# Mixer B: one product with v per four score tiles, 512 columns wide, and put-off work moved to the end of a step

## The chip, the cores and the metric

The kernel runs on one core of a Trainium2 chip. The metric is the device time of one launch in microseconds (us); three runs of the kernel before gave 1504.79, 1506.16 and 1506.5 us, median 1506.16. A core has engines that each work through a list of instructions in order and wait for each other by semaphores: TensorE (PE, matmuls and transposes; PEld is its loading of the stationary operand), VectorE (DVE), ScalarE (ACT), GpSimd (POOL), and SyncE (SP), which here only issues DMAs. [...]

## What is computed

Two layers over 1024 tokens of width 1024: layer 0 with neighbourhood attention (mixer A), layer 1 with grouped-query attention (mixer B), each followed by a dense part (output projection, gated per-layer embedding). The change is in mixer B:

```python
def q_block(qb):                                    # 128 queries, 16 heads, 4 k/v heads
    sc = jnp.einsum('bkgqd,bksd->bkgqs', qb, k).astype(jnp.float32) * scale
    pr = jax.nn.softmax(sc, axis=-1).astype(v.dtype)
    return jnp.einsum('bkgqs,bksd->bkgqd', pr, v)
...
return (o * jax.nn.silu(gate)) @ w_out
```

Every product of float32 accuracy is made of two or three products of rounded operands: an operand x is split into a high part xh (rounded to fp32r) and a rest xl = x - xh.

## The kernel before

The phases run one after the other: mixer A, a dense phase, mixer B, a dense phase. In mixer B (`mixer_b`, lines 1054 to 1382) the attention is 128 steps (`steps`, line 1253). A step is one tile of 128 queries of one head against all 1024 keys: 16 heads in 8 pairs, two halves of the tokens (`hf`), four tiles t in each half, so that four steps in a row belong to one head and half. Each step has three parts:

- `f_S` (scores): four matmuls of 512 columns into a PSUM tile of 128x1024 (two such tiles take turns), and on DVE the minimum of each row, `mn` (line 1265).
- `f_E` (exp): one ACTIVATE on ACT over 128x1024 into P (line 1271), with the sum of each row.
- `f_T`: eight transposes of P on PE (line 1281) into two PSUM tiles of four blocks (`psT` has two buffers, so the transposes of the next step wait until these are read), each copied by ACT to PTh (line 1283) and with the rest taken by DVE to PTl (line 1284).

The parts overlap over steps: the program text of step n holds f_T of n, f_E of n+1 and f_S of n+2. PTh and PTl hold two tiles (256 columns). At every second step, n = 2, 4, 6, ..., `f_AV` (line 1289) multiplies V with both kept tiles: 8 matmuls with PTh and 8 with PTl, each 256 columns wide, into one half of a 512-column PSUM tile `o`. Such a step is called an AV step here, any other a plain step. In an AV step the order is f_AV, f_E, f_T, f_S; in a plain step f_T, f_E, f_S. After the fourth tile `head_end` puts off the work that brings `o` to SBUF (lines 548 and 512). In the middle of some AV steps (`turned`, line 1295) `q_stack` transposes the queries of the next two heads; the copy that brings a head's queries to the rows of the stationary operand QS follows later in two parts, on ACT (line 1244) and on DVE (line 1245).

Between the parts of the steps stands dense work: pieces of projections (q, k and v of later heads, gates, embedding products), 6 matmuls of 512 columns or 12 of 256 each. `mix` (line 372) places them: each entry of the list `att` carries a weight (CB for an AV step, CN for a plain step: weights of turn, f_AV, f_T, f_E, f_S), and after each entry pieces are issued until their share of the total equals the share of the weights done. A step of kind "apart" is given a piece ahead of it if none has come since the last f_T. What brings a piece's PSUM to SBUF (`leave`) may be put off behind the f_E that follows it.

`pulse` (line 351) is called after every entry of `att`. It does two things: `WQ.pump` moves the queue of weights on (a DMA to a staging buffer, then a copy `wh` on ACT, line 230, and the rest `wl` on DVE, line 235; new ones begin only while `WQ.gate` is true, which is between the scores of an odd step and the next `turn`), and `post.tick` counts down all other put-off work (copies, row scalings, DMAs of results) and issues what is due. With `turn`, f_AV, f_E, f_T and f_S as entries a plain step has four pulses and an AV step five.

The 128 steps are given to `mix` in four groups of 32 (g = 0 to 3). By the code group 0 has 24 dense pieces, group 1 has 50, groups 2 and 3 have 32 each. `WQ.gate` is None (always open) from step 112.

Of the kernel before, what the change touches and what calls it, by code (L numbers as in the profile page):

```python
# [12 lines left out]
F32R = mybir.dt.float32r  # L13
# [8 lines left out]
NT = 8  # L22
# [6 lines left out]
SEED = 0x5F3759DF - (1 << 22) - (1 << 31)  # L29
WSLOTS = 4  # L30
CA = (1.0, 0.5, 1.25, 1.0, 0.75)
CB = (1.25, 1.0, 2.0, 0.5, 1.0)
CN = (1.5, 0.0, 1.0, 1.0, 1.5)
DG, DR, DQ, DY, NP = 1, 2, 2, 1, 8
KT, KN = 2, 4
# [125 lines left out]
def trunk(ctx, tc, x, wts, rpb, gains, hgains, mask, sides, rope, gain0, out):  # L161
    nc = tc.nc
# [119 lines left out]
    def load_y(l, t):  # L282
        for i, (d, src) in enumerate(zip((HTh, HTl), yD[l])):
            k0 = 4 if i and t >= 4 else 0
            (act if t < 4 and l else sync).dma_start(d[:, t, k0:7].bitcast(F32), src[t, :, k0:7])
# [34 lines left out]
    def mm(ps, a, b, first, last):  # L320
        pe.matmul(ps, a, b, start=first, stop=last, skip_group_check=True)  # L321
# [29 lines left out]
    def pulse():  # L351
        WQ.pump()
        post.tick()
# [16 lines left out]
    leave = Evac()  # L370
# [683 lines left out]
    def mixer_b(pend):  # L1054
        with ExitStack() as es:
# [3 lines left out]
            one = es.enter_context(tc.tile_pool(name="bone", bufs=1))  # L1059
# [3 lines left out]
            psT = es.enter_context(tc.tile_pool(name="bpt", bufs=2, space=PSUM))  # L1063
            psO = es.enter_context(tc.tile_pool(name="bpo", bufs=1, space=PSUM))

            PTh = one.tile([128, NT, 256], F32R, name="PTh")
            PTl = one.tile([128, NT, 256], F32R, name="PTl")

            def dalloc():
                if pro[0]:  # L1070
# [8 lines left out]
            KA, KB, V, QT, QST, P, RS, OP = {}, {}, {}, {}, {}, {}, {}, {}  # L1079
# [150 lines left out]
            def q_stack(pair, hf):  # L1230
                g = pair // 2
                ps = psT.tile([128, 4, 128], F32, name="t")
                c = slice((pair % 2) * 128, (pair % 2) * 128 + 128)
                for t in range(4):
                    pe.transpose(ps[:, t], QT[g, hf][:, t, c], ident)  # L1235
                raw = sb.tile([128, 512], F32, name="th")
                act.activation(raw, ps.rearrange("p t c -> p (t c)"), AF.Copy)
                for j in range(2):
                    own, oth = slice(64 * j, 64 * j + 64), slice(64 - 64 * j, 128 - 64 * j)
                    qs = sb.tile([128, 512], F32R, name="QS", bufs=3)  # L1240
                    QST[2 * pair + j, hf] = qs

                    def high(qs=qs, own=own, oth=oth):
                        act.activation(qs[own], raw[own], AF.Copy)
                        post.add(DQ, lambda: dve.tensor_tensor(qs[oth], raw[own], qs[own], ALU.subtract))
                    if pro[0]:
                        high()
                    else:
                        post.add(QO[j], high)
# [3 lines left out]
            steps = [(2 * p + j, hf, t) for p in range(8) for hf in range(2) for j in range(2) for t in range(4)]  # L1253

            def f_S(h, hf, t):
                g = h // 4
                ps = psS.tile([128, 1024], F32, name="s")
                qt = QST[h, hf][:, t * 128:(t + 1) * 128]
                for kk, kt in enumerate((KA[g], KB[g])):
                    for c in range(2):  # L1260
                        mm(ps[:, c * 512:(c + 1) * 512], qt, kt[:, c * 512:(c + 1) * 512], kk == 0, kk == 1)
                if t == 0:
                    RS[h, hf] = sb.tile([128, 4], F32, name="rs", bufs=3)
                mn = sb.tile([128, 1], F32, name="mn", bufs=3)
                dve.tensor_reduce(mn, ps, axis=AX.X, op=ALU.min)  # L1265
                P[h, hf, t] = (ps, mn)
# [6 lines left out]

            def f_T(h, hf, t):
                p = P.pop((h, hf, t))
                c = slice((t % 2) * 128, (t % 2) * 128 + 128)
                for b in range(2):
                    ps = psT.tile([128, 4, 128], F32, name="t")
                    for i in range(4):
                        k = 4 * b + i  # L1280
                        pe.transpose(ps[:, i], p[:, k * 128:(k + 1) * 128], ident)  # L1281
                    ks = slice(4 * b, 4 * b + 4)
                    act.activation(PTh[:, ks, c], ps, AF.Copy)  # L1283
                    dve.tensor_tensor(PTl[:, ks, c], ps, PTh[:, ks, c], ALU.subtract)  # L1284
# [1 line left out]
            def talloc():  # L1286
                return psO.tile([128, 512], F32, name="o").rearrange("p (t c) -> p t c", t=4)

            def f_AV(h, hf, t):
                if t == 1:  # L1290
                    OP[h, hf] = psO.tile([128, 512], F32, name="o")
                o = OP[h, hf][:, (t - 1) * 128:(t + 1) * 128]
                for k in range(NT):
                    mm(o, V[h // 4][:, k], PTh[:, k], t == 1 and k == 0, False)
                while turned:
                    turned.pop(0)()
                for k in range(NT):
                    mm(o, V[h // 4][:, k], PTl[:, k], False, t == 3 and k == NT - 1)
                if t == 3:
                    fin = head_end(sb, h, hf, RS[h, hf], OP.pop((h, hf)), ylive, 1, gg, talloc)  # L1300
                    if fin:
                        later.add(FIN[1], fin)
# [18 lines left out]
            def exps(n):  # L1321
                def f():
                    f_E(*steps[n])
                f.first = True
                return f

            def blocks(n):
                def f():
                    f_T(*steps[n])
                f.kind = "apart" if n % 2 else "blocks"  # L1330
                return f
            for g in range(4):
                att = []
                for n in range(32 * g, 32 * g + 32):
                    h, hf, t = steps[n]
                    av = n >= 2 and n % 2 == 0
                    w = CB if av else CN
                    def turn():
                        if WQ.gate:
                            WQ.gate = False  # L1340
                        later.tick()
                    att.append((turn, w[0]))
                    if av:
                        att.append((lambda n=n: f_AV(*steps[n - 1]), w[1]))
                    te = [(blocks(n), w[2])]
                    if n + 1 < len(steps):
                        te.append((exps(n + 1), w[3]))
                    if n % 2 == 0 and n > 0:
                        te.reverse()
                    att += te  # L1350
                    if n + 2 < len(steps):
                        def scores(n=n):
                            f_S(*steps[n + 2])
                            WQ.gate = n % 2 == 1 if n < 112 else None
                        att.append((scores, w[4]))
                    m = n + QS_AT
                    if m % 8 == 0 and m < len(steps):
                        hn, fn, _ = steps[m]
                        att.append((lambda hn=hn, fn=fn: turned.append(lambda: q_stack(hn // 2, fn)), 0.0))
                    if YLOAD_B <= n < YLOAD_B + NT:  # L1360
                        att.append((lambda t=n - YLOAD_B: load_y(1, t), 0.0))
                if g == 3:
                    att.append((lambda: f_AV(*steps[-1]), CB[1]))
                def gates(p):
                    return [i for hf in range(2) for i in gate_items("bg", p, hf, dalloc, sb, gg)]
                dense = []
                if g > 0:
                    dense += left
                if g < 3:
                    qi = q_items(g + 1, pool)  # L1370
                    kv = kv_items(1, pool) if g == 1 else [None, None]
                    dense += kv[:-2] + qi[:KS] + [k for k in kv[-2:-1] if k] + qi[KS:8] + [k for k in kv[-1:] if k] + gates(2 * g + 1) + qi[8:]
                    left = gates(2 * g + 2)
                else:
                    WQ.cap[3] = 2
                    dense += gates(2 * g + 1) + pp_items(1, dalloc, sb, TAGS_B)
                mix(att, dense, hold=HOLD + 1 if g == 3 else 0)
# [442 lines left out]
    mixer_a()  # L1820
    pend = dense_phase(0)
    mixer_b(pend)
    dense_phase(1)

# [17 lines left out]
```

## Time and profile before

| | |
|---|---|
| runs, median (lowest to highest) | 1506.16 us (1504.79 to 1506.5) |
| the profiled execution's own time | 1505.39 us |
| its span, first to last instruction | 1503.6 us |
| PE, DVE, ACT, POOL busy | 98%, 71%, 61%, 31% of the span |
| granted TensorE clock | 0.999 |
| mixer B's 128 steps in the trace | about 762.6 to 1321.6 us |

The span is shorter than the execution by 1.8 us, which lie before its first and behind its last instruction. A busy PE is not PE at its peak, since the ends of pipelined matmuls are modelled; the distance between the starts of matmuls tells how fast PE goes. All rows with times are of this one execution.

### The profile page before, as it was taken

The page shows a single profiled execution, that of the slowest core. Times are in us where ns is not written, and L with a number is a line of the kernel's source. Part 1 is how long each engine was busy: PE and PEld are TensorE (multiplying, and loading weights), DVE is VectorE, ACT ScalarE, POOL GpSimd, SP SyncE. Part 2 cuts the span into 40 slices and gives each one's busy share as a digit, 9 for nine tenths or more (in the row PEclk, how much of TensorE's full clock was granted, in tenths as well). Part 3 has the DMA queues.
Part 4 walks back from the last instruction along what each step waited for, and adds up shares of the span by engine and source line. Part 5 has one row for each costly group of instructions (what it writes and reads, how often), then busy time and mean ns, then how long its engine had stood idle before and what let it go on. Part 6 is the DMA issues. An engine that isn't in the chain of part 4 may idle for free.

```text
span 1503.6 us, 24725 instructions
## 1 busy us (share of the span) xinstructions
PE 1480.6 (98%) x8885; PEld 1304.0 (87%) x8885; DVE 1071.6 (71%) x2042; ACT 917.2 (61%) x1866; POOL 461.0 (31%) x623
## 2 busy tenths in 40 slices
PE   8999999999999999999999999999999999999998
PEld 8888988988988887888988999989999988888886
DVE  7566476477477598756887786777877887689844
ACT  7676476477477535433567776767767777745432
POOL 1456476387265200020322222443131300000123
PEclk9999999999999999999999999999999999999999
DMA  8334374283122863262210111111101122763223
GB/s 257 126 104 131 71 178 139 64 168 100 36 89 85 326 247 99 92 206 80 77 50 22 33 51 39 47 33 44 58 28 48 38 78 66 240 234 114 69 90 135
DMA packets 91242, 157.44 MB, mean 105 GB/s; under 512 B 18160, under 2 KB 54256, under 8 KB 90608
## 3 DMA queue, kind: packets, MB, share of 16 engines
q1 hardware_dynamic: 87120, 143.53, 29.1%
q0 software_dynamic: 2560, 8.39, 3.7%
q10 hardware_dynamic: 1440, 3.94, 0.8%
q8 instruction: 71, 1.16, 0.3%
q14 instruction: 51, 0.42, 0.1%
HBM read 125.30 MB, written 50.83 MB: 117 GB/s over the span
## 4 chain that ended last, share of the span: by engine, by line
PE 51%; DVE 7%; ACT 2%; issue 1%; POOL 0%; ACTq 0%; POOLq 0%; DVEq 0%
PE d L321 25%; PE s L321 9%; PE o L321 8%; PE t L1281 7%; PE t L496 1%; DVE xn L1616 1%; PE t L321 1%; DVE X L1512 1%; DVE PTl L1284 1%; DVE HTl L1458 0%; DVE wl L235 0%; DVE mn L1265 0%; DVE wl L1410 0%; PE t L1235 0%; ACT wh L230 0%
## 5 line engine op out<-in xcount | busy, mean ns | idle before, releaser
L321 PE MATMUL d<-wh,HTh 128*128 128x256 f32 (+1 forms) x1000 | 331.8, 335 | 1.9 <-DVE X L1512 0.6
L321 PE MATMUL d<-wh,HTl 128*128 128x256 f32 (+1 forms) x1000 | 327.7, 331 | 0.4 <-DVE HTl L498 0.4
L321 PE MATMUL d<-wl,HTh 128*128 128x256 f32 (+1 forms) x1000 | 327.0, 330 | 0.3 <-DVE wl L1410 0.2
L1284 DVE TENSOR_TENSOR PTl<-t,PTh 128x512 fp32r<-128x512 f32 x256 | 164.7, 685 | 106.5 <-ACT PTh L1283 106.2
L321 PEld LDWEIGHTS d<-wh,HTh 128*128 128x128 f32 x1000 | 187.8, 189 | 22.2 <-ACT HTh L497 1.5
L321 PEld LDWEIGHTS d<-wl,HTh 128*128 128x128 f32 x1000 | 188.1, 189 | 20.0 <-DVE wl L1410 0.6
L321 PE MATMUL d<-HTh,wh 128*128 128x512 f32 x504 | 204.6, 406 | 0.0
L321 PEld LDWEIGHTS d<-wh,HTl 128*128 128x128 f32 x1000 | 187.9, 189 | 18.9 <-DVE HTl L498 0.6
L321 PE MATMUL d<-HTh,wl 128*128 128x512 f32 x504 | 198.1, 393 | 0.0
L321 PE MATMUL d<-HTl,wh 128*128 128x512 f32 x504 | 197.3, 392 | 0.0
L1271 ACT ACTIVATE P<-s,mn 128x1024 f32<-128x1024 f32 x128 | 142.7, 1115 | 47.3 <-DVE mn L1265 46.4
L1283 ACT ACTIVATE PTh<-t 128x512 fp32r<-128x512 f32 x256 | 139.2, 594 | 46.2 <-PE t L1281 45.7
L1265 DVE TENSOR_REDUCE mn<-s 128x1 f32<-128x1024 f32 x128 | 155.1, 1212 | 9.8 <-PE s L321 9.2
L804 POOL TENSOR_TENSOR PTh<-PTh,SIDE 128x256 fp32r<-128x256 f32 x96 | 81.2, 845 | 192.9 <-ACT PTh L799 192.9
L1281 PE MATMUL t<-ident,P 128*128 128x128 f32 x1024 | 134.8, 273 | 2.6 <-DVE PTl L1284 2.0
L321 PE MATMUL s<-KA,QS 128*128 128x512 f32 (+2 forms) x384 | 134.1, 403 | 1.1 <-DVE mn L778 1.1
L1281 PEld LDWEIGHTS t<-ident,P 128*128 128x128 f32 x1024 | 115.3, 140 | 12.8 <-DVE PTl L1284 6.9
L321 PE MATMUL s<-KB,QS 128*128 128x512 f32 (+2 forms) x384 | 121.5, 370 | 0.0
L235 DVE TENSOR_TENSOR wl<-wstage,wh 128x1024 fp32r<-128x1024 f32 x78 | 97.8, 1255 | 32.8 <-ACT wh L230 32.5
L321 PE MATMUL o<-PTl,V 128*128 128x256 f32 (+2 forms) x672 | 120.0, 290 | 1.1 <-DVE PTl L1284 0.6
L321 PE MATMUL o<-PTh,V 128*128 128x256 f32 (+2 forms) x672 | 118.4, 287 | 1.8 <-DVE Y L512 0.8
L321 PEld LDWEIGHTS d<-HTh,wl 128*128 128x128 f32 x504 | 94.6, 188 | 21.6
(253 smaller groups left out, 2883.3 us busy)
## 6 DMA issues: line engine op xcount, KB each, us to landing
wstage<-in_wts SPq DMA_DIRECT2D x88, 512.0 KB
pp<-ppD SPq DMA_DIRECT2D x32, 256.0 KB
X<-in_x SPq DMA_DIRECT2D x15, 512.0 KB
rb<-rD SPq DMA_DIRECT2D x56, 128.0 KB
ppD<-th SPq DMA_DIRECT2D x20, 256.0 KB
tD0t<-in_wts SPq DMA_DIRECT2D x16, 256.0 KB
tD1t<-in_wts SPq DMA_DIRECT2D x16, 256.0 KB
xD<-X SPq DMA_DIRECT2D x8, 512.0 KB
```

Source lines behind the costliest of these rows:

```text
L235: eng.tensor_tensor(lo[:, c:c + n], s[:, c:c + n], hi[:, c:c + n], ALU.subtract)
L321: pe.matmul(ps, a, b, start=first, stop=last, skip_group_check=True)
L496: pe.transpose(ps[:, k], xn[:, (4 * c + k) * 128:(4 * c + k + 1) * 128], ident)
L804: pool.tensor_tensor(pt[:, 3 * j - 1:3 * j + 4:4], pt[:, f1:f1 + 1].to_broadcast([128, 2, 128]), SIDE[:, :2], ALU.mult)
L1265: dve.tensor_reduce(mn, ps, axis=AX.X, op=ALU.min)
L1271: act.activation(p, ps, AF.Exp, bias=mn, scale=-1.0, accum_out=RS[h, hf][:, t:t + 1])
L1281: pe.transpose(ps[:, i], p[:, k * 128:(k + 1) * 128], ident)
L1283: act.activation(PTh[:, ks, c], ps, AF.Copy)
L1284: dve.tensor_tensor(PTl[:, ks, c], ps, PTh[:, ks, c], ALU.subtract)
L1512: dve.tensor_tensor(xt, ps, xt, op)
L1616: dve.scalar_tensor_tensor(xn, X[t], rn[m][:, i:i + 1], g1, op0=ALU.mult, op1=ALU.mult)
```

## The change

`f_AV` runs once in four steps with all four tiles, each matmul 512 columns wide; PTh and PTl are twice as large (512 columns). The last head is done in two halves, at step 126 and behind step 127, as it was before. AV steps are n = 4, 8, ..., 124 and 126. A step's f_T, f_E and f_S become one entry of `att`, with no dense piece between them and no pulse until f_S is issued; then follow two pulses within the entry and that of `mix`, so the number of pulses in a step stays the same. "Apart" are now all plain steps but those with n a multiple of four. No entry has the mark `first` any more, so what brings a dense piece's PSUM to SBUF is not put off. An AV step's weights sum to 0.5, a plain step's to 5.0 as before. The build option `dynamic_dma_scratch_size` is set to 2048.

```diff
@@ -29,7 +29,7 @@
 SEED = 0x5F3759DF - (1 << 22) - (1 << 31)
 WSLOTS = 4
 CA = (1.0, 0.5, 1.25, 1.0, 0.75)
-CB = (1.25, 1.0, 2.0, 0.5, 1.0)
+CB = (0.0, 0.0, 0.0, 0.0, 0.5)
 CN = (1.5, 0.0, 1.0, 1.0, 1.5)
 DG, DR, DQ, DY, NP = 1, 2, 2, 1, 8
 KT, KN = 2, 4
@@ -1063,8 +1063,8 @@
             psT = es.enter_context(tc.tile_pool(name="bpt", bufs=2, space=PSUM))
             psO = es.enter_context(tc.tile_pool(name="bpo", bufs=1, space=PSUM))
 
-            PTh = one.tile([128, NT, 256], F32R, name="PTh")
-            PTl = one.tile([128, NT, 256], F32R, name="PTl")
+            PTh = one.tile([128, NT, 512], F32R, name="PTh")
+            PTl = one.tile([128, NT, 512], F32R, name="PTl")
 
             def dalloc():
                 if pro[0]:
@@ -1273,7 +1273,7 @@
 
             def f_T(h, hf, t):
                 p = P.pop((h, hf, t))
-                c = slice((t % 2) * 128, (t % 2) * 128 + 128)
+                c = slice(t * 128, t * 128 + 128)
                 for b in range(2):
                     ps = psT.tile([128, 4, 128], F32, name="t")
                     for i in range(4):
@@ -1286,17 +1286,18 @@
             def talloc():
                 return psO.tile([128, 512], F32, name="o").rearrange("p (t c) -> p t c", t=4)
 
-            def f_AV(h, hf, t):
-                if t == 1:
+            def f_AV(h, hf, a=0, b=4):
+                if a == 0:
                     OP[h, hf] = psO.tile([128, 512], F32, name="o")
-                o = OP[h, hf][:, (t - 1) * 128:(t + 1) * 128]
+                c = slice(a * 128, b * 128)
+                o = OP[h, hf][:, c]
                 for k in range(NT):
-                    mm(o, V[h // 4][:, k], PTh[:, k], t == 1 and k == 0, False)
+                    mm(o, V[h // 4][:, k], PTh[:, k, c], a == 0 and k == 0, False)
                 while turned:
                     turned.pop(0)()
                 for k in range(NT):
-                    mm(o, V[h // 4][:, k], PTl[:, k], False, t == 3 and k == NT - 1)
-                if t == 3:
+                    mm(o, V[h // 4][:, k], PTl[:, k, c], False, b == 4 and k == NT - 1)
+                if b == 4:
                     fin = head_end(sb, h, hf, RS[h, hf], OP.pop((h, hf)), ylive, 1, gg, talloc)
                     if fin:
                         later.add(FIN[1], fin)
@@ -1327,13 +1328,13 @@
             def blocks(n):
                 def f():
                     f_T(*steps[n])
-                f.kind = "apart" if n % 2 else "blocks"
+                f.kind = "apart" if n % 4 and n != 126 else "blocks"
                 return f
             for g in range(4):
                 att = []
                 for n in range(32 * g, 32 * g + 32):
                     h, hf, t = steps[n]
-                    av = n >= 2 and n % 2 == 0
+                    av = n == 126 or n >= 4 and n % 4 == 0
                     w = CB if av else CN
                     def turn():
                         if WQ.gate:
@@ -1341,18 +1342,23 @@
                         later.tick()
                     att.append((turn, w[0]))
                     if av:
-                        att.append((lambda n=n: f_AV(*steps[n - 1]), w[1]))
+                        att.append((lambda n=n: f_AV(*steps[n - 1][:2], 0, 4 if n < 126 else 2), w[1]))
                     te = [(blocks(n), w[2])]
                     if n + 1 < len(steps):
                         te.append((exps(n + 1), w[3]))
-                    if n % 2 == 0 and n > 0:
+                    if av:
                         te.reverse()
-                    att += te
-                    if n + 2 < len(steps):
-                        def scores(n=n):
+                    def step(n=n, fs=[f for f, _ in te]):
+                        for f in fs:
+                            f()
+                        if n + 2 < len(steps):
                             f_S(*steps[n + 2])
                             WQ.gate = n % 2 == 1 if n < 112 else None
-                        att.append((scores, w[4]))
+                        pulse()
+                        leave.run()
+                        pulse()
+                    step.kind = te[0][0].kind if not av else "blocks"
+                    att.append((step, w[2] + w[3] + w[4]))
                     m = n + QS_AT
                     if m % 8 == 0 and m < len(steps):
                         hn, fn, _ = steps[m]
@@ -1360,7 +1366,7 @@
                     if YLOAD_B <= n < YLOAD_B + NT:
                         att.append((lambda t=n - YLOAD_B: load_y(1, t), 0.0))
                 if g == 3:
-                    att.append((lambda: f_AV(*steps[-1]), CB[1]))
+                    att.append((lambda: f_AV(*steps[-1][:2], 2, 4), CB[1]))
                 def gates(p):
                     return [i for hf in range(2) for i in gate_items("bg", p, hf, dalloc, sb, gg)]
                 dense = []
@@ -1831,7 +1837,7 @@
     from concourse.bass_utils import run_bass_kernel_spmd
 
     arrays = {n: np.ascontiguousarray(a) for n, a in lay_out(inputs).items()}
-    nc = bacc.Bacc("TRN2", target_bir_lowering=False, num_devices=1)
+    nc = bacc.Bacc("TRN2", target_bir_lowering=False, num_devices=1, dynamic_dma_scratch_size=2048)
     aps = [nc.dram_tensor(f"in_{n}", arrays[n].shape, mybir.dt.from_np(arrays[n].dtype), kind="ExternalInput").ap()
            for n in NAMES]
     aps.append(nc.dram_tensor("out", (NT, 128, D), F32, kind="ExternalOutput").ap())
```

## Prediction: what the change does to the time

> **What bounds the kernel now.** I read the page's busy times and its chain of work first, then the busy times by stretch, one for each of mixer B's four groups of 32 steps.
>
> ```profile
> span 1503.6 us, 24725 instructions
> PE 1480.6 (98%) x8885; PEld 1304.0 (87%) x8885; DVE 1071.6 (71%) x2042; ACT 917.2 (61%) x1866; POOL 461.0 (31%) x623
> PE 51%; DVE 7%; ACT 2%; issue 1%; POOL 0%; ACTq 0%; POOLq 0%; DVEq 0%
> ```
>
> ```profile
> 762.60:889.00 126.40, 126.08 (x893) 114.94 (x892) 98.65 (x153) 93.78 (x173) 28.82 (x42) 1.00 0.11 30
> 889.00:1050.30 161.30, 159.97 (x1146) 148.32 (x1145) 116.93 (x200) 109.84 (x219) 62.99 (x112) 1.00 0.15 44
> 1050.30:1185.30 135.00, 135.00 (x947) 124.90 (x946) 105.11 (x166) 96.23 (x178) 33.81 (x48) 1.00 0.14 42
> 1185.30:1321.60 136.30, 132.70 (x834) 115.58 (x832) 103.19 (x149) 101.81 (x179) 11.12 (x10) 1.00 0.35 114
> ```
>
> The columns are the stretch, its length, then busy PE, PEld, DVE, ACT, POOL, the clock and DMA. PE is busy all through, at full clock, and heads the chain: a nanosecond taken from PE's list is a nanosecond of the time, and a wait of PE is lost. DVE at 103.19 of 136.30 and ACT at 101.81 are three quarters full, so a burst on either can reach PE. How long does PE wait in mixer B now? The waits of its two queues there:
>
> ```profile
> PEld t L1281 <- DVE PTl L1284: 6.9, 17, 1.3
> PEld o L321 <- ACT PTh L1283: 2.7, 4, 0.9
> ...
> PE t L1281 <- DVE PTl L1284: 2.0, 3, 0.9
> PE o L531 <- DVE Y L512: 0.8, 1, 0.8
> PE o L321 <- DVE Y L512: 0.8, 2, 0.5
> ```
>
> (total us, times, longest). Most are transposes (t) that wait until DVE has emptied their PSUM tile: two f_T close together. The rows shown add to 13.2 us; the two queues can overlap in them, so I take 10 us as lost, between 3.6 (the PE rows alone) and 13.2.
>
> **Term 1: wider products.** The work:
>
> ```profile
> L321 PE MATMUL o<-PTl,V 128*128 128x256 f32 x512 | 73.2, 285 | 0.6 <-DVE PTl L1284 0.6
> L321 PE MATMUL o<-PTh,V 128*128 128x256 f32 x512 | 72.0, 283 | 1.2 <-DVE Y L512 0.8 <-ACT PTh L1283 0.4
> ```
>
> 1024 matmuls of 256 columns. By the diff 31 of the 32 head halves become 16 matmuls of 512 columns instead of 32 of 256 (the last stays in two halves): 992 become 496. The mean of 285 ns is a latency; the cost is the distance of starts, from PE's timeline:
>
> ```profile
> 1070.48 1.03 PE L1281 MATMUL t<-ident,P 128*128 128x128 f32 x8
> 1071.27 0.71 PE L321 MATMUL s<-KA,QS 128*128 128x512 f32 x2
> 1071.82 0.63 PE L321 MATMUL s<-KB,QS 128*128 128x512 f32 x2
> 1072.28 0.39 PE L321 MATMUL d<-HTh,wh 128*128 128x512 f32 x1
> ...
> 1073.65 1.12 PE L321 MATMUL o<-PTh,V 128*128 128x256 f32 x8
> 1074.60 1.12 PE L321 MATMUL o<-PTl,V 128*128 128x256 f32 x8
> 1075.56 1.04 PE L1281 MATMUL t<-ident,P 128*128 128x128 f32 x8
> ```
>
> Sixteen products of 256 columns take 1075.56 - 1073.65 = 1.91 us, 119.4 ns each. The dense piece (six of 512, same kind of operands) takes 1073.65 - 1072.28 = 1.37 us, 228 ns each; the second pair of scores 0.46 us, 230 ns each. Two narrow ones cost 238.8, one wide one 228 to 230: 9 to 11 ns saved. 496 x 10.4 = **5.2 us saved** (4.4 to 5.4). PE runs in order, so nothing covers this and nothing takes it back.
>
> [...]
>
> **Term 2: waits that go.** f_T now nearly always has either a dense piece or the whole f_AV between it and the f_T before (group 0, the sparsest, has 24 pieces for 25 plain steps), and put-off work no longer stands on DVE between a step's transposes and its PTl. So the t waits, 6.9 + 2.0 by the rows, should mostly go. One PSUM tile `o` serves four steps instead of being refilled two steps after its predecessor, so the `o <- Y` wait should go too. The waits at the end (last AV, last transposes) stay, since their order stays. Of 10 us I take **6 us gone** (0 to 10).
>
> **Term 3: waits that come.** From the weights of `mix`, four steps of groups 0, 2 and 3 now read: f_AV f_T f_S, piece f_T f_S, piece f_T f_S, piece f_T f_S, with what is left over ahead of f_AV; group 1 mostly has two pieces for one. So plain steps follow each other at one piece's distance: 0.79 (t) + 1.01 (s) + 1.37 = 3.17 us from the rows above. f_AV takes 3.7 us and gives every engine time, but the plain steps before it come in threes. Two chains must fit into 3.17. The rows of ACT and DVE around the same steps (f_T at 1067.29 and 1070.48):
>
> ```profile
> 1068.12 1.08 ACT L1283 ACTIVATE PTh<-t 128x512 fp32r<-128x512 f32 x2
> 1069.23 0.59 ACT L548 ACTIVATE Y<-o 64x512 f32<-64x512 f32 x1
> 1069.72 0.62 ACT L1244 ACTIVATE QS<-th 64x512 fp32r<-64x512 f32 x1
> 1071.12 1.08 ACT L1283 ACTIVATE PTh<-t 128x512 fp32r<-128x512 f32 x2 [0.78 <-PE t L1281]
> 1072.23 0.63 ACT L1244 ACTIVATE QS<-th 64x512 fp32r<-64x512 f32 x1
> 1072.88 1.12 ACT L1271 ACTIVATE P<-s,mn 128x1024 f32<-128x1024 f32 x1
> 1073.90 0.19 ACT L1271 ACTIVATION_READ_ACCUMULATOR P<-s,mn 128x1 f32 x1
> ```
>
> ```profile
> 1071.75 1.29 DVE L1284 TENSOR_TENSOR PTl<-t,PTh 128x512 fp32r<-128x512 f32 x2
> 1073.07 0.69 DVE L1245 TENSOR_TENSOR QS<-th,QS 64x512 fp32r<-64x512 f32 x1
> 1073.79 1.23 DVE L1265 TENSOR_REDUCE mn<-s 128x1 f32<-128x1024 f32 x1
> ```
>
> *Queries.* The DVE half of a head pair's first QS stands here between PTl and mn. The pulse counts (4 for the ACT half, then 2) put it, after the change, at the first pulse behind f_S of the step after f_AV, so behind mn: mn then starts at 1073.07, ends at 1074.29, and QS at 1074.98. The scores that read it are two steps ahead, in the next step; that step is plain now, not an AV step, so they are due at 1070.48 + 3.17 + 0.79 = 1074.44. PE is blocked about 0.5 us; behind these scores wait all dense pieces and transposes. This comes once in eight steps where one piece stands between: 4 times in groups 0 and 2 each, 3 in group 3, 1 in group 1. 12 x 0.5 = **6 us lost** (0 to 14, if up to 0.7 us of other DVE work is due first, as the join of L512 can be).
>
> *Exp and weights.* f_T of n+1 needs f_E of n+1, which stands on ACT behind PTh of n. From f_T at 1070.48: PTh from 1071.12 to 1072.20, and an exp directly behind it would end 1.12 later, at 1073.32, so 2.84 us, some 2.95 with the semaphore: 0.2 of slack. Put-off work on ACT lies behind exp now, in the idle 0.6 us before the next PTh, but a weight copy is longer:
>
> ```profile
> L230 ACT ACTIVATE wh<-wstage 128x1024 fp32r<-128x1024 f32 x17 | 18.0, 1057 | 0.3 <-issue 0.3
> ```
>
> 17 in mixer B; all fell into steps followed by an AV step, now about half fall between two plain ones. Some 6 of these lie outside group 1, at 1.06 - 0.6 - 0.2 = 0.3, or 0.9 where a dense piece's copy comes too: **2 us lost** (0 to 6).
>
> Costed at nothing: the order of DMAs on SP (weights, row sums, results) keeps its sequence, moved by at most a step's part, while the first three stretches move 30 to 44 GB/s and the last 114; where a weight came late, the dense piece and all PE behind it would wait. The first PTh copy of a new group of four lies behind f_AV on PE anyway, so the single PTh buffer adds no wait. f_AV right behind f_S reads PTh first and now spends 1.84 us there before it needs PTl, which covers PTl better than the 0.95 of before.
>
> **Sum**, against the profiled execution (1505.39, its span 1503.6 and 1.8 around it): -5.2 - 6 + 6 + 2 = -3.2, so 1502.2. The median of the runs is 0.8 above that execution; between 1502.2 and 1503.0 I take **1502.5**. The saving is small because PE was never slowed by the number of products, only by 10 ns for each, and the better spacing pays with a new wait.
>
> **The rivals.**
>
> 1. *The queries come in time.* If DVE is ahead of my sum, or the steps stand wider apart, the 6 us do not come: 1496.5. For it: exp may already hold f_T back and so hide this wait. Against it: QS starts behind mn in the list, whatever else happens.
> 2. *ACT's loop of copy and exp becomes the bound* (slower). Two of three plain steps in a row depend on exp in the step before; groups 0, 2 and 3 have 24 fours, so 48 such f_T. If copies of dense pieces, no longer put off behind exp, lengthen the loop from 2.95 to 3.4 us, each is 0.23 late: 11 us, so 1513.5. It decides from 3.25 us on, where 48 x 0.08 eats the gain. For it: ACT is at 101.81 of 136.30 and 0.6 us copies stand right there. Against it: the loop has 0.6 us of idle time in which the shorter ones fit.
> 3. *A wide product is worth two narrow ones, or the old waits only change their names.* Either takes away most of the gain: about 1506. Against the first: the 228 of the rows.
> [...]
>
> **How the numbers follow.** Forecast 0.45, rival 1 0.15, rival 2 0.20, rival 3 0.17, rival 4 0.03. A measurement can tell about 0.2%, 3 us, from no change. The forecast's own range, from the bounds of its waits, is 1497 to 1507: of its 0.45 about 0.27 lie below 1503.1 (3 us under the median), 0.16 within 3 us of it and 0.02 above. With rival 1 this gives faster 0.42; with rival 3 (0.16 within, 0.01 above) same 0.32; the rest, with rivals 2 and 4, gives slower 0.26. The range, 1495.5 to 1512, takes in rival 1 and most of rival 2.
>
> **What would show it.** Term 1: 496 products of 512 columns at 228 to 232 ns from start to start. Term 2: t no longer waits for PTl more than a few times, and o not for Y. Term 3: a wait of PE's scores for the QS of L1245, about 12 times 0.5 us, and transposes that wait for P in the second and third plain step. Wrong would be: a wide product over 236 ns, no wait for QS, transposes waiting for P by more than 5 us in all, or a mixer A longer than before.

## Result: slower by 0.7%, and the profile after

The changed kernel took 1518.2 us in the median of six runs (1516.14 to 1520.72), the kernel before 1506.33 (1504.79 to 1510.03) in six runs beside it: a ratio of 1.007, with a 95% interval of 1.0058 to 1.0083. The forecast was 1502.5 with a range of 1495.5 to 1512; the time lies above both. The profiled execution of the changed kernel has a span of 1515.2 us, 11.6 more than the 1503.6 of before. Ratios compare runs at a granted clock of 0.995 to 0.999; one run of the last experiment, 1653.94 us at a granted clock of 0.829, is left out. The head of the changed kernel's page:

```profile
span 1515.2 us, 23551 instructions
PE 1480.3 (98%) x8389; PEld 1275.8 (84%) x8389; DVE 1073.2 (71%) x2042; ACT 918.1 (61%) x1866; POOL 464.4 (31%) x623
...
PE 47%; DVE 9%; ACT 3%; issue 2%; POOL 1%; DMA 0%; SPq 0%; ACTq 0%; POOLq 0%; DVEq 0%
```

PE has 496 matmuls fewer, and its share of the chain of work that ended last fell from 51 to 47% while that of DVE, ACT and POOL rose: waits took the place of products. Busy times of the four groups of mixer B, in the columns of the prediction's view (the stretches begin with the same instruction as there):

```profile
763.40:888.60 125.20, 123.33 (x758) 106.85 (x757) 100.15 (x156) 94.06 (x175) 31.06 (x42) 1.00 0.10 30
888.60:1058.50 169.90, 161.49 (x1017) 141.54 (x1016) 117.19 (x195) 109.57 (x218) 63.48 (x112) 1.00 0.14 41
1058.50:1195.70 137.20, 135.17 (x818) 117.49 (x817) 104.67 (x169) 97.60 (x179) 36.55 (x48) 1.00 0.14 41
1195.70:1330.90 135.20, 131.75 (x722) 109.11 (x720) 103.32 (x147) 100.06 (x176) 10.04 (x10) 1.00 0.35 113
```

Groups 0 and 3 are 1.2 and 1.1 us shorter than before, group 2 is 2.2 longer, and group 1, the one with 50 dense pieces, went from 161.3 to 169.9: 8.6 longer. The waits of PE's weight loads in mixer B say for what (total us, times, longest):

```profile
PEld s L321 <- DVE QS L1245: 6.9, 12, 0.9
PEld t L1281 <- ACT P L1271: 4.8, 9, 1.5
PEld d L321 <- ACT th L1203: 3.6, 5, 0.7
PEld t L1167 <- issue: 2.2, 1, 2.2
PEld d L321 <- ACT G L604: 2.2, 2, 1.1
PEld d L321 <- ACT qt L1147: 2.1, 3, 0.7
PEld t L1281 <- issue: 1.6, 3, 0.8
PEld t L1281 <- DVE PTl L1284: 1.5, 4, 0.8
PEld d L321 <- ACT th L635: 1.5, 2, 1.2
```

New are scores that wait for QS (12 times, 6.9 us), transposes that wait for P (4.8), and something that the forecast has no word on: dense pieces (`d`) that wait for ACT, 3.6 + 2.2 + 2.1 + 1.5 = 9.4 us; before, all their waits were 1.2 us. The `t <- PTl` row went from 6.9 to 1.5, but PE's own row for the same wait did not fall; before it was 2.0, and now it is

```profile
PE t L1281 <- DVE PTl L1284: 2.1, 4, 1.1
```

A weight load that waits for several things is put down to one of them, so part of the wait for PTl now stands under other names: "issue", and "P" (the experiment with the weight copies shows such a place). All rows of the PEld view, with five smaller ones that are not shown, add to 30.7 us, those of the kernel before to 14.7. That is 16.0 more, less the 5.3 us by which the products became shorter: 10.7 of the 11.6. The sum fits better than it can be trusted: a weight load can wait while products still run, and PE's own rows in the same stretches add to 16.1 and 5.1, which would leave 5.7.

The products themselves, from PE's timeline:

```profile
929.23 2.00 PE L321 MATMUL o<-PTh,V 128*128 128x512 f32 x8
931.07 1.98 PE L321 MATMUL o<-PTl,V 128*128 128x512 f32 x8
932.88 1.03 PE L1281 MATMUL t<-ident,P 128*128 128x128 f32 x8
```

Sixteen wide products take 932.88 - 929.23 = 3.65 us, 228 ns each, against 238.8 for two narrow ones.

The dense pieces' wait, first on PE, then on ACT in the same time:

```profile
921.50 0.28 PE L321 MATMUL d<-wh,HTl 128*128 128x256 f32 x1
922.30 0.39 PE L321 MATMUL d<-wh,HTh 128*128 128x256 f32 x1 [0.52 <-ACT th L1203]
```

```profile
920.24 1.12 ACT L1271 ACTIVATE P<-s,mn 128x1024 f32<-128x1024 f32 x1
921.25 0.19 ACT L1271 ACTIVATION_READ_ACCUMULATOR P<-s,mn 128x1 f32 x1
921.87 0.39 ACT L1203 ACTIVATE th<-d 128x256 f32<-128x256 f32 x1 [0.42 <-ACT P L1271]
```

One piece ends a projection tile with the matmul at 921.50; ACT, idle, copies the tile out from 921.87 on; the next piece, which opens a new tile, should start at 921.62 and starts at 922.30, 0.68 later. The pool of `d` (line 1062; in PSUM, where PE writes its results and from where ACT copies this one in 0.39 us) has one buffer, so the next tile can't begin before the copy of the last one is done. Before the change a step's transposes or scores stood between two pieces and covered that time. With the three parts made one entry, `mix` can only put the second piece right behind the first: PE's list has 16 places in group 1 with two pieces side by side, and at ten of them a new tile begins and waits (7.9 of the 9.4 us; the other two waits, 1.5, stand behind the last step).

### The profile page after: what moved, and what is told of

Same layout as the page of the kernel before. It is cut to its first block, busy times and chain, and to the rows that moved or that the text cites. A ratio compares the mean times of both kernels' runs of the same rounds, so it can differ in the third digit from the quotient of the medians.

```text
span 1515.2 us, 23551 instructions
## 1 busy us (share of the span) xinstructions
PE 1480.3 (98%) x8389; PEld 1275.8 (84%) x8389; DVE 1073.2 (71%) x2042; ACT 918.1 (61%) x1866; POOL 464.4 (31%) x623
## 4 chain that ended last, share of the span: by engine, by line
PE 47%; DVE 9%; ACT 3%; issue 2%; POOL 1%; DMA 0%; SPq 0%; ACTq 0%; POOLq 0%; DVEq 0%
PE d L321 23%; PE s L321 8%; PE o L321 8%; PE t L1281 5%; DVE PTl L1284 2%; DVE mn L1265 1%; PE t L496 1%; ACT PTh L1283 1%; DVE xn L1622 1%; PE t L321 1%; DVE X L1518 1%; DVE QS L1245 1%; DVE HTl L1464 0%; DVE wl L1416 0%; PE t L1235 0%
## 5 line engine op out<-in xcount | busy, mean ns | idle before, releaser
L321 PE MATMUL o<-PTl,V 128*128 128x512 f32 (+3 forms) x424 | 112.3, 357 | 0.7 <-DVE mn L778 0.2
L321 PE MATMUL o<-PTh,V 128*128 128x512 f32 (+3 forms) x424 | 111.1, 354 | 1.0 <-POOL PTh L804 0.8
```

## The experiments

The main theory was that the loss is made of single waits that add: QS, the one PSUM tile `d`, P, and the stacks of q and k. Its main rival was the forecast's second rival, ACT's loop of copy and exp as the bound, with the other waits only standing in for it. Each ratio below is to the kernel before on the same chip; the kernel before had medians of 1506.33 to 1508.45 in the sets, so ratios, not times, are compared. The waits are sums of the PEld rows in mixer B, in us, under the names that the profile gives them.

| kernel | ratio (95%) | s for QS | d for ACT | t for P | t for PTl | k_stack |
|---|---|---|---|---|---|---|
| before | 1 | 0 | 1.2 | 0 | 6.9 | 0 |
| changed | 1.0070 (1.0058 to 1.0083) | 6.9 | 9.4 | 4.8 | 1.5 | 3.0 |
| e1_qs_early | 1.0041 (1.0028 to 1.0054) | 0 | 9.3 | 7.0 | 1.5 | 3.5 |
| e2_g1_split | 1.0010 (0.9996 to 1.0025) | 6.2 | 5.2 | 6.1 | 1.5 | 1.6 |
| e3_split_all | 1.0002 (0.9990 to 1.0014) | 0 | 4.1 | 14.9 | 0.9 | 1.6 |
| e4_narrow_lump | 1.0046 (1.0030 to 1.0061) | 0.6 | 6.7 | 0 | 3.2 | 0 |
| e5_both | 0.9982 (0.9973 to 0.9992) | 0 | 5.1 | 7.0 | 1.5 | 1.9 |
| e6_gate | 0.9957 (0.9943 to 0.9972) | 0 | 5.1 | 4.9 | 1.5 | 1.9 |
| e7_halves | 1.0124 (1.0107 to 1.0140) | 7.2 | 9.4 | 4.9 | 1.6 | 3.1 |
| e8_piece | 0.9947 (0.9932 to 0.9962) | 0 | 3.8 | 2.1 | 1.0 | 2.7 |
| e9_best_halves | 0.9993 (0.9981 to 1.0005) | 0 | 3.8 | 2.9 | 1.1 | 2.7 |
| e10_kstack | 0.9944 (0.9924 to 0.9965) | 0.3 | 3.7 | 2.2 | 0.9 | 3.1 |

### The queries' copy earlier

```diff
-QO = (4, 6)
+QO = (2, 4)
```

> The changed kernel with the two halves of the queries' copy (QS) counted down from 2 and 4 pulses instead of 4 and 6, so that the DVE half of the first head is issued in the AV step and not one step later. Main theory (the loss is made of single waits that add up: 12 waits of scores for QS, 7 us; 10 waits of a dense piece for the one PSUM tile d, 8 us; transposes waiting for P, 5 us; q/k stacks, 3 us): no wait of s for QS of L1245 is left, and the time falls by 6 to 7 us, from 1518 to about 1511.5, so still above the 1506 of before. Rival (ACT's loop of copy and exp is the bound, the wait for QS only covers it): the QS wait goes, waits of t for P of L1271 grow by as much, and the time stays at 1516 to 1518.

1.0041 instead of 1.0070: 0.29%, 4.4 us. In the changed kernel the wait looks like this, on PE and on DVE:

```profile
1084.21 1.03 PE L1281 MATMUL t<-ident,P 128*128 128x128 f32 x8
1085.50 0.73 PE L321 MATMUL s<-KA,QS 128*128 128x512 f32 x2 [0.25 <-DVE QS L1245]
```

```profile
1082.31 1.29 DVE L1284 TENSOR_TENSOR PTl<-t,PTh 128x512 fp32r<-128x512 f32 x2
1083.51 1.21 DVE L1265 TENSOR_REDUCE mn<-s 128x1 f32<-128x1024 f32 x1
1084.76 1.40 DVE L1245 TENSOR_TENSOR QS<-th,QS 64x512 fp32r<-64x512 f32 x2
```

The scores were due 0.79 us behind the transposes, at 1085.00; the first QS copy, behind mn, ended at about 1085.46. With the earlier count, on DVE of this experiment:

```profile
1079.38 0.68 DVE L1245 TENSOR_TENSOR QS<-th,QS 64x512 fp32r<-64x512 f32 x1
1080.09 0.68 DVE L512 SCALAR_TENSOR_TENSOR Y<-o,Y 64x512 f32<-64x512 f32 x1
1080.70 1.27 DVE L1284 TENSOR_TENSOR PTl<-t,PTh 128x512 fp32r<-128x512 f32 x2
```

the first QS is done before the next step's PTl, and no scores wait for it. Of the 6.9 us 2.2 come back as longer waits for P: the truth lies between the theories, nearer the first.

### The parts of a step apart in group 1

```diff
+                    if g == 1:
+                        att += te
+                        if n + 2 < len(steps):
+                            def scores(n=n):
...
+                            att.append((scores, w[4]))
+                    else:
                     def step(n=n, fs=[f for f, _ in te]):
```

> The changed kernel, but in group 1 (steps 32 to 63) f_T, f_E and f_S are entries of their own again, with a pulse after each, so that dense pieces can stand between them; the wide products stay. Main theory: of 14 places where two pieces stand next to each other in group 1 two are left, so the 8 us of PE's waits d for ACT's th, G and qt go to 1 or 2, the one QS wait in this group goes too (0.8 us), and the time falls by 7 to 9 us, to about 1510. Rival (ACT's loop is the bound everywhere): a quarter of the steps is changed, so at most a quarter of 12 us, 3 us, comes back: 1515.

1.0010: 0.6% of the 0.7%, 9 us and uncertain by 3, most of the whole loss from a quarter of the steps, as the theory of single waits had it and not that of ACT's loop. The d waits fell from 9.4 to 5.2, not to the 1 or 2 that were expected; by PE's own rows, which leave out what running products cover, they fell from 6.1 to 1.5. The wait of the k stacks fell from 3.0 to 1.6.

### The parts apart in all groups

The same without the condition, so that no step is lumped; the wide products stay.

> The changed kernel with the entries f_T, f_E and f_S apart in all four groups, as in the kernel before; wide products and the weights of the changed kernel stay. Main theory: QS waits (7 us) and nearly all d waits (7 of 8 us) go; the waits of t for PTl that the kernel before had come back in part (2 to 4 us): 1506 to 1508. If wide products were themselves no gain (the rival of a wide product that costs two narrow ones), it would be 1511 or more; with the spacing of 228 ns that the trace of the changed kernel shows it can't be. Rival (ACT's loop): the copies of dense pieces still stand ahead of PTh, so waits of t for P stay at 5 us or more and the time at 1513 or more.

1.0002, inside the expected range, but not for the reason given: `t <- PTl` did not come back (0.9), while waits for P tripled. The rival had these waits right, but not its time of 1513 or more. Its rows show what lumping had been good for; first PE's waits, then ACT and PE around step 69:

```profile
PEld t L1281 <- ACT P L1271: 14.9, 23, 1.9
```

```profile
1073.93 1.09 ACT L1283 ACTIVATE PTh<-t 128x512 fp32r<-128x512 f32 x2 [0.94 <-PE t L1281]
1075.05 0.63 ACT L1244 ACTIVATE QS<-th 64x512 fp32r<-64x512 f32 x1
1075.70 1.12 ACT L1271 ACTIVATE P<-s,mn 128x1024 f32<-128x1024 f32 x1
```

```profile
1076.96 1.09 PE L1281 MATMUL t<-ident,P 128*128 128x128 f32 x8 [0.34 <-ACT P L1271]
```

With a pulse between f_T and f_E a put-off copy (QS) gets between PTh and exp, so that P is done late, and the transposes of the next plain step, due 3.17 us after those of this one (1073.30), come at 1076.96, 0.5 late. So the chain of copy and exp is as tight as the forecast said, and keeping put-off work out of it is worth something; lumping does that, but it pays in the other two places.

### Narrow products, parts in one entry

The kernel before with only the `step` entry of the change, at its own weights.

> The kernel before (products of 256 columns at every second step, its own weights) with only the entries f_T, f_E and f_S made one, and the pulses behind f_S. Main theory: two pieces stand next to each other at 16 places of group 1, about half of them across the change of the PSUM tile d, which costs 8 x 0.8 = 6 us; the scores that need a new QS now follow an AV step, whose 1.9 us cover the copy, so no QS wait: 1510 to 1513. Rival (the lumping is harmless, the threes of plain steps that wide products bring are what costs): 1504 to 1507, with no d waits.

1.0046, 6.9 us slower than before, a little more than expected: lumping alone costs, with 6.7 us of d waits and hardly any for QS (0.6). One further wait of 4.0 us in the profiled execution, which at 1518.57 us is the slowest of its five runs, belongs to another chain, shown at the end; whether the other runs have it is not known.

### Both mends together

e1 and e2 in one kernel.

> Both mends together: the copies of QS counted down from 2 and 4 pulses, and in group 1 the three parts of a step apart again. If the waits for QS and the waits of pieces for the PSUM tile d are separate losses, their returns add: from 1.007 of the kernel before, 0.4% by the early QS (measured 1.0041) goes on top of the 1.001 of the split group: about 0.997, 4 to 5 us faster than before. Rival (each wait only uncovers the next, ACT's copy and exp behind it): 1.000 or more, and the waits of t for P grow from 6 to 10 us or more.

0.9982: faster than before by 0.18%. The expectation had taken 0.4% for the earlier QS; with the 0.29% that e1 measured the sum is 1.0010 - 0.0029 = 0.9981, so the two returns add. Waits for P stay at 7.0 us, as in e1.

### New weight copies only ahead of f_AV

```diff
-                                WQ.gate = n % 2 == 1 if n < 112 else None
+                                WQ.gate = n % 4 == 3 if n < 112 else None
```

> As the one with both mends, and in the lumped groups new weight copies may begin only behind the scores of steps 3, 7, 11, ..., which an AV step follows, not behind every odd step. If weight copies on ACT between plain steps are what makes transposes wait for P (up to 1.2 us at steps 38, 66, 99), 1 to 3 us more come back than with the two mends alone: 0.995 to 0.997. Rival (weights now come too late): dense pieces wait for wh or wl, and it is slower than that one.

0.9957, 0.25% or 3.8 us better, uncertain by 2.7; the rows for P went from 7.0 to 4.9, and no wait for weights appeared. PE's own rows tell what went: there P stays at 2.2 us, and it is PTl that falls from 1.5 to 0.3. The changed kernel has the same place, the transposes of step 99, here on DVE, ACT, PEld and PE:

```profile
1203.15 2.58 DVE L235 TENSOR_TENSOR KB<-wstage,KA 128x1024 fp32r<-128x1024 f32 x2
1205.66 1.27 DVE L1284 TENSOR_TENSOR PTl<-t,PTh 128x512 fp32r<-128x512 f32 x2
1204.39 1.15 ACT L1271 ACTIVATE P<-s,mn 128x1024 f32<-128x1024 f32 x1
1206.45 0.42 PEld L1281 LDWEIGHTS t<-ident,P 128*128 128x128 f32 x4 [1.54 <-ACT P L1271]
1206.48 0.63 PE L1281 MATMUL t<-ident,P 128*128 128x128 f32 x4 [1.15 <-DVE PTl L1284]
```

P is done at 1205.54, 0.9 us before the load that is said to wait for it. What ends last is the first half of PTl, which stood behind the rests of two weight copies (2.58 us) on DVE. The transposes were due at 1205.18 (the last product of a piece at 1204.95, and 0.23), so P alone would have cost them some 0.4 us of the 1.3 that they come late. What the narrower gate takes away is in the main DVE's part of the weight copies, not ACT's.

### One piece from group 1 to group 0

```diff
                     left = gates(2 * g + 2)
+                    if g == 0:
+                        dense.append(left.pop(0))
```

> As the one with both mends and the narrower gate, and one gate piece moved from group 1 to group 0, so that step 31 too has a piece between scores and transposes. The wait of 1.0 to 1.35 us for P at step 31 should go, about 1 us (0.07%) less than the one with the gate, which is below what a comparison can tell; the trace is to show it. If pieces in group 1 fall worse by it (the order of pieces there shifts by one), d waits grow and nothing is won.

0.9947. The time can't be told from 0.9957; the trace shows the wait at step 31 gone and P at 2.1 us in all. This is the best version tried, 0.5% faster than the kernel before.

### Each wide product as two narrow ones

```diff
-                    mm(o, V[h // 4][:, k], PTh[:, k, c], a == 0 and k == 0, False)
+                    for i in range(a, b, 2):
+                        d = slice(i * 128, i * 128 + 256)
+                        mm(OP[h, hf][:, d], V[h // 4][:, k], PTh[:, k, d], i == 0 and k == 0, False)
```

(PTl alike.) In the changed kernel:

> The changed kernel with each product of 512 columns issued as two of 256, all else as in the changed kernel. It prices the wide product alone: by the spacing in the traces (228 against 2 x 119.5 ns, 496 times) it is 5.3 us slower than the changed kernel, 1.0105 of the kernel before. [...]

In the best version:

> The best version so far (both mends, narrower gate, one piece moved; 0.9947 of the kernel before) with each product of 512 columns issued as two of 256, all else the same. If the wide product's worth is PE's own time (496 x 10.6 ns), it is 5.3 us slower than the best version here too, where few waits are left: 0.998 of the kernel before. Rival (the wide product's worth is mostly in the spacing around it, as the 0.54% of the first try in the changed kernel, 8 us, may say): 1.000.

1.0124 against 1.0070, and 0.9993 against 0.9947: 0.54 and 0.46%, 8 and 7 us, each uncertain by some 3 us. The 5.3 us by the spacing lie within that; no saving at all, as in the prediction's third rival, does not. The traces narrow it: from its first transposes to the `rb` product behind its last step (line 531), mixer B takes 573.11 us in e7 against 566.80 in the changed kernel, and 555.38 in e9 against 548.60 in the best version, 6.3 and 6.8 us more. All PEld waits together grew by 0.7 and 1.1 us of that, which leaves some 5.6, near the 5.3. Without the wide products the best version would be level with the kernel before.

### The k stacks two pieces later

```diff
-                    dense += kv[:-2] + qi[:KS] + [k for k in kv[-2:-1] if k] + qi[KS:8] + [k for k in kv[-1:] if k] + gates(2 * g + 1) + qi[8:]
+                    dense += kv[:-2] + qi[:6] + [k for k in kv[-2:-1] if k] + qi[6:8]
+                    gt = gates(2 * g + 1)
+                    dense += gt[:2] + [k for k in kv[-1:] if k] + gt[2:] + qi[8:]
```

> The best version so far with the two transposes of k (k_stack) issued two pieces later. They wait there for POOL's and DVE's work (1.5 and 0.9 us of PE). If it is the work on the last k tiles that is late, two pieces (2.8 us and the steps between) cover it and 2 us come back: 0.9935. Rival (they wait for the PSUM tile t that the step's own transposes hold, wherever they stand behind f_S): the waits stay near 1 us each and the time at 0.9947.

0.9944, the same. PE and DVE of this experiment show why:

```profile
986.66 1.04 PE L1281 MATMUL t<-ident,P 128*128 128x128 f32 x8
989.05 0.63 PE L1167 MATMUL t<-ident,qt 128*128 128x128 f32 x4 [1.35 <-DVE PTl L1284]
```

```profile
988.21 1.29 DVE L1284 TENSOR_TENSOR PTl<-t,PTh 128x512 fp32r<-128x512 f32 x2 [1.55 <-ACT PTh L1283]
```

The stack stands right behind a step's own transposes, which hold both PSUM tiles `t`, and the first is free when DVE has read it. It is the rival that holds in this version: two pieces later in the list change nothing, as long as a step's own transposes stand directly ahead. In the changed kernel the profile puts the longest wait of a k stack (1.84 us) down to POOL's work, so there the cause stays open.

## Why the prediction was wrong

**Term 1, the wider products: right.** 228 ns each, as expected, 5.2 us forecast and 5.3 by the trace; e7 and e9 put it at 7 to 8 with 5.3 inside their uncertainty, and their traces at some 5.6.

**Term 2, waits that go: near in size, half right in kind.** The rows of products that wait in `o` went from 5.6 to 2.7 us, and `o` no longer waits for Y in the middle of the phase. Transposes waiting for PTl fell from 6.9 to 1.5 us by PEld's rows alone. With the waits that PE's rows put down to PTl and PEld's to something else (1.54 us at step 99, 0.60 and 0.77 at steps 66 and 67) it is 4.4. The old waits, two f_T close together, went; new ones came where rests of weight copies and other small DVE work, now behind mn, hold up the next step's PTl. Of the 6 us some 5 went, by these rows.

**Term 3, queries: right.** 12 waits, 6.9 us by PEld's rows and 4.0 by PE's, against 12 and 6 forecast; taking them away gave 4.4 us (e1).

**Term 3, exp and weights: too small, and in part another wait.** 2 us were forecast, and the trace has 4.8 under the name of P, of which 1.54 end with PTl. Weight copies between plain steps were priced for ACT; what the gate (e6) took back was in the main their rests on DVE, which the forecast gave no price. Not priced either was the step without a piece (step 31, 1.2 us), which e8 shows.

**The step that failed** is the sentence "group 1 mostly has two pieces for one". It was read as a larger distance between plain steps, which helps both chains, and so group 1 was counted as safe. Where the second piece writes its results was not asked: `d` is one PSUM tile, and a piece that opens a new tile right behind one that closes its own must wait for ACT's copy, some 0.8 us each by PEld's rows (9.4 us in 12 waits, ten of them in group 1). That is 8 us more (9.4 against 1.2), a wait that the sum had at nothing, and e2 brought the loss nearly to zero by putting transposes or scores between the pieces again, in group 1 alone. The rule was there to be read: the pool's one buffer, and the order of the pieces, of which the kernel before has none side by side in group 1. To the same step belongs the k stack, 3.0 us, which now follows scores or transposes without a piece ahead; e2 halved it.

**The rivals.** The second (ACT's loop, 1513.5) has the right direction, but it isn't the mechanism: t waits for P by 4.8 us at most, not 11, and e2 and e1 together give back the whole loss without touching it (e5). It was the mechanism of e3 (14.9 us). The fourth (the smaller scratch, 0.03) stood at 1519, by an estimate of the author's: each of POOL's 32 DMAs in mixer A held up by the 5.1 us of the view of before, 163 us in all, a tenth of it reaching PE. No run shows that these DMAs use the scratch, and with the smaller one they were not held up: POOL's issues took as long as before, and mixer B's first transposes start at 763.4 instead of 762.6. So 1519 lies nearest to the 1518.2 measured by chance alone. The issues before, then after:

```profile
L661 POOL DMA_DIRECT2D tD0t<-in_wts x8: 766/798/1074, 135.1 to 182.0; - x8
L661 POOL DMA_DIRECT2D tD1t<-tD1t x8: 794/1342/1951, 318.9 to 338.0; - x8
DMA to landing us min/median/max: 3.8/5.1/7.2
```

```profile
L661 POOL DMA_DIRECT2D tD0t<-in_wts x8: 759/794/1062, 135.1 to 182.0; - x8
L661 POOL DMA_DIRECT2D tD1t<-tD1t x8: 807/1339/1958, 319.4 to 338.4; - x8
```

The 2 us or so behind the last step (one piece more is left over to the end, and it too waits for `d`) were not forecast either.

## What to carry to other kernels

When small units of work are lumped into larger ones, look at what the filler between them was covering: here the parts of a step, standing between two pieces of dense work, hid the emptying of a PSUM tile that has only one buffer, and two such pieces side by side, where the second begins a new tile, cost some 0.7 us each time, and ten of them more than the wider products saved. Read a wait in PE's rows and in those of its weight loads before naming its cause: here, at step 99, they named two different engines, ACT and DVE. For each operand that is made "some pulses later", name the instruction that first reads it and count the time again, since a shift that is nearly harmless ahead of a product of 1.91 us (QS in e4, 0.6 us of waits) is a wait ahead of a short step (6.9 us in the changed kernel). With both mended the kernel is 0.2% faster than before, with the narrower gate and the moved piece 0.5%; nearly all of this is the wide products' saving.

## What the runs showed of the hardware that was not expected

In e4 one wait of PE grew to 3.8 us. On SP the DMA of a weight (line 213) waited until DVE had emptied its staging buffer, and the reload of row sums (line 521) waited for their store. The store of an embedding product (line 636) stood behind both, and ACT could not reuse the tile `th` before it had landed. SP's waits, then ACT's and PE's:

```profile
SPq L213 <- DVE wl L235: 15.7, 1, 15.7
SPq L521 <- DMA rD<-r8T: 3.9, 1, 3.9
```

```profile
1278.34 0.60 ACT L635 ACTIVATE th<-d 128x512 f32<-128x512 f32 x1 [5.75 <-DMA ppD<-th]
1279.62 1.11 PE L1281 MATMUL t<-ident,P 128*128 128x128 f32 x4 [3.77 <-ACT th L1237]
```

And the stretches of e4 around PE's wait, in the columns of before (PE busy first, the clock third from the end):

```profile
1276.00:1279.60 3.60, 0.00 (x0) 0.00 (x0) 0.00 (x0) 1.23 (x3) 1.26 (x1) 0.75 0.53 180
1279.60:1284.60 5.00, 4.98 (x14) 4.12 (x15) 3.16 (x5) 3.15 (x6) 0.00 (x0) 0.50 0.14 52
1284.60:1290.00 5.40, 5.40 (x37) 4.83 (x36) 3.85 (x6) 4.99 (x9) 0.00 (x0) 0.99 0.18 68
```

After the wait PE ran for 5 us at a granted clock of 0.50: one long wait cost itself and, by an estimate from these rows (half of 5 us), some 2.5 us more. It is one such wait in one run; that the wait brought the clock down is read from the order of the rows alone. In the changed kernel, whose longest wait of PE in mixer B is 1.8 us, the four stretches all show 1.00.
